# Three more query and key projections by Strassen, ahead of attention, and elementwise sums handed to accumulating DMAs

## The chip, the cores and the metric

The kernel runs on one core of a Trainium2 chip. The metric is the device time of one execution in microseconds, the median of several runs. Before the change it was 1445.59 us (three runs, 1443.7 to 1447.14).

## The reference: what is computed

One layer of a hybrid encoder on x of 1024 tokens by 1024 channels, all in float32: a token mixer with two branches, an output projection and a layer norm, then a SwiGLU network and a second layer norm. The change lies in the mixer:

```python
proj = x @ w_in                       # split into q_a, k_a, v_a, f_a, q_b, f_b, i_b, g_b, gate_a, gate_b
# branch A, 8 heads of 64: causal softmax attention with forget gates
F = cumsum(log_sigmoid(f_a + b_f))
s[t, u] = q_t . k_u / sqrt(64) + F[t] - F[u]      # u <= t
y_a = softmax(s) @ v
# branch B (HGRN2), 4 heads of 128: S_t = diag(f_t) S_(t-1) + k_t v_t^T, o_t = S_t^T q_t
f = lb + (1 - lb) * sigmoid(f_b); q = silu(q_b); k = 1 - f
# then an RMS norm of o, a sigmoid gate, and
merged = sigmoid(gate_a) * (y_a @ w_pa) + sigmoid(gate_b) * (y_b @ w_pb)
mix = merged @ w_o
```

## The kernel before, in words

**Arithmetic.** A product of two float32 matrices is made of three matmuls in the fast format float32r: each operand is split into a high part (a cast by ACT) and a low part (a subtraction by DVE), and high x high, high x low and low x high are summed in PSUM (`mm3`, line 449; `split`, line 420). A unit is one 128x128 block of weights against 512 tokens.

**Strassen.** Large products are made by Winograd's form of Strassen's scheme: of a 2 x 2 block product seven products are made in place of eight, with sums of blocks before and after. The quarters A11 to A22 of x and the sums S1 to S4 are kept as split operands in `vops` (line 489 on). S1 stands in the place of A21, which is restored later (`split4(A21, a21)`).

**Stages.** First the values of both branches (v, Strassen), with the forget gates. Then `qk_first` (line 720) makes queries and keys of head pair 0 by Strassen. Then for each of four pairs `attention(p, qk)` (line 763), and after each of the first three `qk_project` (line 708): the plain product, 8 blocks of 128 channels, for q and for k, in two halves of 512 tokens, each followed by `qk_heads`, which splits the result out of PSUM into q2, k2 and kl for the pair's two heads. After the fourth pair stands `hgrn_project(0)` (line 856), then for four heads `hgrn` (line 884). The gates follow: four plain ones (`gate`, line 1032; PSUM tile gps) and the first halves of others (`gate_part`, line 1047; ge), then the rest by Strassen (gs), the branch outputs' projections (pps), the output projection (o), and the SwiGLU network (fa, fb, fc, then p).

**Attention** of one head: the negated gate sums nf are broadcast by a DMA into one row of box1, and DVE adds the causal constant to a second row (line 773). For each of eight blocks of 128 queries (qb): two matmuls per score chunk, a DVE instruction that adds the gate sums and keeps the minimum, an exponential by ACT that also sums the row, a reciprocal by DVE and a scaling by POOL. After qb 3 and 7 (g = 0, 1) the probabilities are transposed by PE, split again into th and tl, and multiplied by the values (pv).

**HGRN** of one head: fk = f (line 888), its logarithm, running sums b by blocks; then six levels (`level`, line 925) with block lengths from 64 to 2. Each takes the difference e of b and its value at the block's middle (DVE, line 931), two exponentials by ACT, two products by DVE, four matmuls (lp) and a masked copy. `states` (line 971) makes the decayed keys kd likewise from a difference (line 974) and carries the states between blocks.

**Order.** Every call goes through `Plan` (line 57), which does not issue it at once but records it with the tiles it reads and writes and a cost in nanoseconds by engine and size (`cost`, line 131). `schedule` (line 170) then places the calls greedily: of all calls that are ready, the one with the earliest start, ties by a rank of lateness, on five queues (PE, ACT, DVE, POOL, and SP for all DMAs). A tile's buffer is one of a tag's fixed number (`BUFS`, line 378; `SPREAD`, line 30, for PSUM banks), taken in the order of the tag's list. The resulting order of each engine is fixed in the program; on the chip only semaphores hold it. Matmuls of gates and projections thus stand between those of attention and of HGRN wherever the plan found a place. A matmul that depends on another engine is planned with 400 ns of slack (`SLACK`, line 37).

Of the kernel before, what the change touches and what calls it, by code (L numbers as in the profile page):

```python
# [37 lines left out]
SWITCH = 300.0  # L38
ALPHA = 2.0 ** 0.25
# [16 lines left out]

class Plan:
# [4 lines left out]
    OWN = {"PE": 0.0, "ACT": 0.0, "DVE": 127.0, "POOL": 60.0, "SP": 2500.0}  # L62
    SETS = {AF.Exp: 0, AF.Ln: 0, AF.Sigmoid: 1, AF.Silu: 2}

    def __init__(self, tc):
        self.tc = tc
        self.calls, self.tiles, self.log, self.first = [], {}, {}, {}
        self.queues, self.rank = {}, []
        self.early = 0
        self.loose = set()  # L70
# [23 lines left out]
    def add(self, q, method, args, kw):  # L94
        outs, ins = [], []
        flat = list(args) + [v for k, v in kw.items() if k != "accum_out"]
        for i, v in enumerate(flat):
            if isinstance(v, bass.AP):
                (outs if i == 0 else ins).append(v)
        if "accum_out" in kw:  # L100
            outs.append(kw["accum_out"])
        if method == "copy_predicated":
            ins.append(outs[0])
        n = len(self.calls)
        self.rank.append(n - self.early)
        pred = set()
        names = set()
        for writes, aps in ((False, ins), (True, outs)):
            for ap in aps:
                name, b = self.box(ap)  # L110
                bank = str(ap.space).endswith("PSUM")
                names.add(name)
                seen = self.log.setdefault(name, [])
                keep = []
                for e in seen:
                    m, w, c = e
                    hit = c[0] < b[1] and b[0] < c[1] and c[2] < b[3] and b[2] < c[3]
                    if hit and m != n and (w or writes or bank and self.calls[m][0] is not q):
                        pred.add(m)
                    if not (writes and m != n and b[0] <= c[0] and c[1] <= b[1] and b[2] <= c[2] and c[3] <= b[3]):  # L120
                        keep.append(e)
                keep.append((n, writes, b))
                self.log[name] = keep
        fresh = sorted(x for x in names if x in self.tiles)
        for name in fresh:
            self.tiles[name][2] += 1
            self.first.setdefault(name, n)
        both = sum(str(v.space).endswith("SB") and v.free_size() > 128 for v in ins) > 1
        self.calls.append((q, method, args, kw, pred, names, fresh, self.cost(q.name, method, outs, ins, kw), both))

    def cost(self, eng, method, outs, ins, kw):
# [27 lines left out]
        if eng == "POOL":  # L159
            if method == "tensor_tensor" and kw.get("op") == ALU.pow:  # L160
# [9 lines left out]
    def schedule(self, slack, wait):  # L170
# [13 lines left out]
        dma_free = 0.0  # L184
        fifo, slots = {}, {}
# [15 lines left out]
        while done < len(calls):  # L201
            best = None
            for q, av in avail.items():
                for i in av:
# [38 lines left out]
            else:  # L243
# [6 lines left out]
                fin = t + d  # L250
                free[q] = fin
# [35 lines left out]
    def lag(self, i, u, slack):  # L287
        q, uq = self.calls[i][0].name, self.calls[u][0].name
        lat = self.OWN[q] if uq == q else self.LAT[q]
# [4 lines left out]
    def latest(self, slack):  # L294
# [7 lines left out]
        for old, i in self.after:  # L302
            for m in by.get(old, ()):
                users[m].append((i, self.LAT[calls[m][0].name] + 60))
# [62 lines left out]
def trunk(ctx: ExitStack, tc, a: dict, out: bass.AP):  # L367
# [299 lines left out]
    causal = const("causal", [P, 2, P], BF16, "mask")  # L667
# [52 lines left out]
    def qk_first():  # L720

        g, u = (take("hl", [KC, P], f"w{n}0_r") for n in "qk")
        for b, t in enumerate((g, u)):
            sync.dma_start(t, a["w_qk"][b, 0])
        b11, b12, b21, b22 = g[:, :4], u[:, :4], g[:, 4:], u[:, 4:]
        t2 = take("ph", [4, P], "wqk_t2")
        p1, u2, p5 = (half("ph", f"qk0_{i}") for i in ("p1", "u2", "p5"))
        oa, ob, oc = (bank(t, f"qk0_{t}") for t in ("s", "pt", "s"))
        tiles = qk_tiles(0)

        def mul(p, src, o, first):
            T = [take(f"w{x}0" if p in ("p6", "p2", "p7") else "tt", [4, P], f"Tqk{p}{x}", F32R) for x in "hl"]
            split(*T, src)
            more = {} if first else {"skip_group_check": True}
            for c in range(4):
                mm3(o, T[0][:, c], T[1][:, c], vops[p][0][c], vops[p][1][c], first and c == 0, c == 3, more)
# [4 lines left out]
        split4(A21, a21)  # L741
        mul("p1", b11, oa, True)
        act.copy(p1, oa)
        mul("p2", b21, oa, False)
        dve.tensor_sub(t2, b22, b12)
        qk_heads(0, 0, oa, *tiles)
        mul("p6", t2, ob, True)
        dve.tensor_add(u2, ob, p1)
        mul("p3", b22, oc, False)
        dve.tensor_add(u2, oc, u2)  # L750
        qk_heads(1, 0, u2, *tiles)
# [4 lines left out]
        qk_heads(1, 1, p5, *tiles)  # L756
# [3 lines left out]
        qk_heads(0, 1, p1, *tiles)  # L760
        return tiles

    def attention(p, qk):
        q2, k2, kl = qk
        for i in range(2):
# [12 lines left out]
            for qb in range(NT):  # L778
                n = (qb + 1) * P
                pt = full("pf", f"p{h}_{qb}") if qb > 3 else half("ph", f"p{h}_{qb}")  # L780
                soft = small([P, 5], "soft")
                mn, sm, rs = soft[:, :3], soft[:, 3:4], soft[:, 4:]
# [101 lines left out]
    def hgrn(h, qfg, box):  # L884
# [3 lines left out]
        dve.tensor_scalar(fk, fk, olb[:, h:h + 1], lb[:, h:h + 1], op0=ALU.mult, op1=ALU.add)  # L888
# [36 lines left out]
        def level(li):  # L925
# [5 lines left out]
            dve.tensor_sub(e.rearrange("p (n t) -> p n t", t=2 * L), bv,  # L931
                           bv[:, :, L - 1:L].to_broadcast([P, nb, 2 * L]))
# [75 lines left out]
        for hf in range(2):  # L1008
            op = bank("pv", f"op{h}_{hf}")
            ss, rr = (lambda t: (t[:, :4], t[:, 4:]))(small([P, 8], "ss"))  # L1010
# [52 lines left out]
    for p in range(4):  # L1063
        attention(p, qk)
        if p < 3:
            qk = qk_project(p + 1)
# [593 lines left out]
def _constants():  # L1660
    import ml_dtypes
# [3 lines left out]
    causal = np.stack([causal, causal.T], axis=1).astype(ml_dtypes.bfloat16)  # L1665
# [89 lines left out]
```

## Time and profile before

| what | value |
|---|---|
| median of 3 runs | 1445.59 us |
| lowest, highest | 1443.7, 1447.14 us |
| profiled execution, first to last instruction (span) | 1441.5 us |
| mean granted TensorE clock | 0.998 |
| moved by DMA | 181.30 MB, mean 126 GB/s |

The profile records one execution by its span; what lies around the span is not in it, and the median of the runs is 4.1 us longer. In its rows PE is the tensor engine's matmuls and PEld its weight loads, DVE the vector engine, ACT the scalar engine, POOL GpSimd, SP the queue that issues the DMAs. A row of a group gives the operation, output and input tiles by the program's names, shapes, count, then busy time in all and the mean in ns of one, then the idle time of the engine just before these instructions and who ended it. A row of waits gives who waited for whom: microseconds in all, times, longest. All calls are issued at line 363, so rows are told apart by their tiles, not their lines.

### The profile page before, as it was taken

The page shows a single profiled execution, that of the slowest core. Times are in us where ns is not written, and L with a number is a line of the kernel's source. Part 1 is how long each engine was busy: PE and PEld are TensorE (multiplying, and loading weights), DVE is VectorE, ACT ScalarE, POOL GpSimd, SP SyncE. Part 2 cuts the span into 40 slices and gives each one's busy share as a digit, 9 for nine tenths or more (in the row PEclk, how much of TensorE's full clock was granted, in tenths as well). Part 3 has the DMA queues.
Part 4 walks back from the last instruction along what each step waited for, and adds up shares of the span by engine and source line. Part 5 has one row for each costly group of instructions (what it writes and reads, how often), then busy time and mean ns, then how long its engine had stood idle before and what let it go on. Part 6 is the DMA issues. An engine that isn't in the chain of part 4 may idle for free.

```text
span 1441.5 us, 18901 instructions
## 1 busy us (share of the span) xinstructions
PE 1430.0 (99%) x6782; PEld 1188.2 (82%) x6782; DVE 1112.8 (77%) x1952; ACT 668.6 (46%) x1167; POOL 87.2 (6%) x100
## 2 busy tenths in 40 slices
PE   9999999999999999999999999999999999999997
PEld 7788888888888888788888888888888888888886
DVE  8998778567998999845857997666677776798596
ACT  5547768667767663344511443323333334434330
POOL 0002213120100110000000000000000000000011
PEclk9999999999999999999999999999999999999999
DMA  7022212211111455858500233233333326977632
GB/s 270 32 89 67 95 60 74 63 60 51 38 59 46 153 170 164 255 181 290 176 0 2 102 95 124 96 110 110 110 110 110 97 92 201 346 276 235 209 129 85
DMA packets 74029, 181.30 MB, mean 126 GB/s; under 512 B 8384, under 2 KB 9792, under 8 KB 73936
## 3 DMA queue, kind: packets, MB, share of 16 engines
q1 hardware_dynamic: 73936, 180.11, 37.9%
q8 instruction: 53, 0.87, 0.3%
q14 instruction: 40, 0.33, 0.1%
HBM read 139.90 MB, written 40.17 MB: 125 GB/s over the span
## 4 chain that ended last, share of the span: by engine, by line
PE 97%; DVE 2%; DMA 1%; issue 0%; ACT 0%; SPq 0%; DVEq 0%; ACTq 0%
PE p L363 14%; PE fb L363 12%; PE bps L363 9%; PE fc L363 8%; PE fa L363 8%; PE o L363 6%; PE pps L363 6%; PE gs L363 5%; PE vx L363 4%; PE gps L363 3%; PE s L363 2%; PE pv L363 2%; PE qps L363 2%; PE kps L363 2%; PE vy L363 2%; PE pt L363 2%
## 5 line engine op out<-in xcount | busy, mean ns | idle before, releaser
L363 PE MATMUL p<-dp 128*128 128x512 f32 (+1 forms) x957 | 210.1, 382 | 0.0
L363 PEld LDWEIGHTS p<-dp 128*128 128x128 f32 x957 | 175.1, 188 | 34.8
L363 PE MATMUL fc<-xs,Tp 128*128 128x512 f32 x528 | 127.3, 389 | 0.6 <-ACT Tp L363 0.6
L363 PE MATMUL fb<-xs,Tp 128*128 128x512 f32 x528 | 127.2, 389 | 0.0
L363 PEld LDWEIGHTS fc<-xs,Tp 128*128 128x128 f32 x528 | 99.1, 188 | 21.6 <-ACT Tp L363 1.0
L363 PEld LDWEIGHTS fb<-xs,Tp 128*128 128x128 f32 x528 | 99.1, 188 | 20.5
L363 PE MATMUL fa<-x,Tp 128*128 128x512 f32 x480 | 115.6, 389 | 0.0
L363 ACT CAST Tp<-t 128x512 fp32r<-128x512 f32 x88 | 54.2, 619 | 118.8 <-PE fc L363 64.8
L363 DVE TENSOR_TENSOR Tp<-t,Tp 128x512 fp32r<-128x512 f32 x88 | 60.6, 690 | 60.5 <-ACT Tp L363 59.9
L363 PEld LDWEIGHTS fa<-x,Tp 128*128 128x128 f32 x480 | 90.1, 188 | 18.7
L363 PE MATMUL bps<-xh,wb_h 128*128 128x512 f32 x192 | 76.2, 397 | 0.0
L363 PE MATMUL bps<-xl,wb_h 128*128 128x512 f32 x192 | 76.0, 396 | 0.0
L363 PE MATMUL bps<-xh,wb_l 128*128 128x512 f32 x192 | 75.5, 396 | 0.0
L363 POOL TENSOR_TENSOR norm<-norm,mhalf 128x1 f32<-128x1 f32 x16 | 17.2, 1075 | 886.3 <-DVE norm L363 886.3
L363 ACT CAST dp<-dap 128x1024 fp32r<-128x1024 f32 (+1 forms) x42 | 41.0, 979 | 57.8 <-PE p L363 35.7
L363 POOL TENSOR_SCALAR p<-p,soft 128x384 f32<-128x384 f32 (+4 forms) x64 | 51.9, 817 | 261.0 <-DVE soft L363 235.2
L363 DVE TENSOR_TENSOR tl<-pt,th 128x512 fp32r<-128x512 f32 (+1 forms) x96 | 52.2, 554 | 19.7 <-ACT th L363 15.5
L363 ACT CAST th<-pt 128x512 fp32r<-128x512 f32 (+1 forms) x96 | 45.5, 479 | 34.9 <-PE pt L363 30.8
L363 DVE TENSOR_TENSOR dp<-dap,dp 128x1024 fp32r<-128x1024 f32 (+1 forms) x42 | 47.4, 1132 | 15.9 <-ACT dp L363 15.7
L363 PE MATMUL fb<-x,Tp 128*128 128x512 f32 x240 | 57.7, 389 | 0.0
L363 PE MATMUL pt<-ident,p 128*128 128x128 f32 x288 | 53.8, 273 | 0.0
L363 ACT CAST Tp<-wg_r 128x512 fp32r<-128x512 f32 x40 | 24.9, 623 | 62.1 <-PE fb L363 30.2
(565 smaller groups left out, 3476.6 us busy)
## 6 DMA issues: line engine op xcount, KB each, us to landing
dbp<-in_w_fo SPq DMA_DIRECT2D x45, 512.0 KB, 5.3
dap<-a_d SPq DMA_DIRECT2D x35, 512.0 KB, 4.3
wg_r<-in_w_ff SPq DMA_DIRECT2D x22, 512.0 KB, 4.0
wu_r<-in_w_ff SPq DMA_DIRECT2D x22, 512.0 KB, 3.6
a_d<-ar SPq DMA_DIRECT2D x42, 256.0 KB, 2.7
a_d<-as SPq DMA_DIRECT2D x33, 256.0 KB, 3.4
wg_r<-in_w_g SPq DMA_DIRECT2D x16, 512.0 KB, 4.4
sg<-gate_d SPq DMA_DIRECT2D x32, 256.0 KB, 3.4
```

The costliest lines, as they stand in the source:

```text
L363: getattr(q.engine, method)(*args, **kw)
```

## The change

Three things are changed together, and the planner is taught about the new kind of call.

1. `qk_project` is gone. `qk_first` now runs `qk_strassen` for the pairs 1, 2, 3 and 0, one after the other, before the first attention. Pair 0's results go to `qk_heads` as before; those of pairs 1 to 3 are written to the DRAM buffer `qk_d`. Before each later attention `qk_load` reads each half back, twice into one tile so that both halves of the partitions hold it, and ACT and DVE split it.
2. The sums with a broadcast are made by DMAs that add into their destination, issued by POOL: the masked gate sums (SP loads the float32 constant, the DMA adds the gate sums), the decay differences e and the decayed keys' exponents kd (ACT writes the negated broadcast, the DMA adds b).
3. The reciprocals and scalings of the score blocks are gathered: three blocks together, then the fourth. f is made by ACT in place of DVE.

The planner counts 1.0 us of POOL for such a DMA, 2.3 us and the bytes at 200 GB/s until it has landed, and at most three in flight. The core of the diff:

```diff
+RING = 3
+    SOFT, LANDS = 1000.0, 2300.0
+        self.lands.append(self.LANDS + o_bytes(outs[0]) / 200.0 if q.name == "POOL" and method == "dma_start" else 0.0)
...
+                    if self.lands[i]:
+                        t = max(t, ring[-RING])
...
-    causal = const("causal", [P, 2, P], BF16, "mask")
...
-    def qk_project(p):
-        tiles = qk_tiles(p)
-        for b in range(2):
-            plan.early = AHEAD
-            w = weights(a["w_qk"][b, p], [KC, P], f"w{'qk'[b]}{p}", 0)
-            plan.early = 0
-            for hf in range(2):
-                o = bank("g", f"{'qk'[b]}ps{p}_{hf}")
-                project(o, w, hf)
-                qk_heads(b, hf, o, *tiles)
-        return tiles
+    def qk_strassen(p, wtags, btags, tiles=None):
+        g, u = (take(t, [KC, P], f"w{n}{p}_r") for t, n in zip(wtags, "qk"))
...
+        def put(b, hf, o):
+            if tiles:
+                return qk_heads(b, hf, o, *tiles())
+            if o is oa:
+                t = half("gt", f"qk{p}_o")
+                act.copy(t, o)
+                o = t
+            sync.dma_start(qk_d[p, b, :, hs(hf)], o)
...
         mul("p5", b12, oc, True)
         act.copy(p5, oc)
-        split4(A21, a21)
+        if tiles:
+            split4(A21, a21)
...
+    def qk_load(p):
+        q2, k2, kl = qk_tiles(p)
+        for b in range(2):
+            for hf in range(2):
+                for i in range(2):
+                    ot = slice((1 - i) * DH, (2 - i) * DH)
+                    raw = half(f"w{'hl'[i]}0", f"qkr{p}_{b}{hf}{i}")
+                    for j in range(2):
+                        sync.dma_start(raw[j * DH:(j + 1) * DH], qk_d[p, b, i * DH:(i + 1) * DH, hs(hf)])
+                    if b == 0:
+                        act.activation(q2[i][:, hs(hf)], raw, AF.Copy, scale=-0.125)
+                        dve.scalar_tensor_tensor(q2[i][ot, hs(hf)], raw[ot], -0.125, f(q2[i])[ot, hs(hf)],
+                                                 op0=ALU.mult, op1=ALU.subtract)
+                    else:
+                        act.copy(k2[i][:, hs(hf)], raw)
+                        dve.tensor_sub(kl[i][:, hs(hf)], raw, f(k2[i])[:, hs(hf)])
+        return q2, k2, kl
...
+        for p, w, b in ((1, "hl", 0), (2, "kb", 1), (3, "hl", 0), (0, "kb", 1)):
+            qk_strassen(p, (w, w), (("s", "pt", "s"), ("h", "pv", "h"))[b], None if p else tiles)
...
-            for hf in range(2):
-                plain, masked = (nfx[:, b0 + 4 * hf:b0 + 4 * hf + 4].rearrange("p (j c) t -> p j c t", c=2) for b0 in (0, NT))
-                dve.tensor_add(masked, plain, causal[:, None].to_broadcast([P, 2, 2, P]))
+            sync.dma_start(box1[:, r + 1, :], a["causal"])
+            pool.dma_start(box1[:, r + 1, :], nf_d[h].partition_broadcast(P), accum_op=ALU.add)
...
-                dve.reciprocal(rs, sm)
-                pool.tensor_scalar(pt[:, :n], pt[:, :n], rs, 1.0, op0=ALU.mult, op1=ALU.mult)
                 pr.append(pt)
+                if qb % 4 > 1:
+                    lo = 0 if qb % 4 == 2 else 3
+                    dve.reciprocal(sums[:, 4 + lo:5 + qb % 4], sums[:, lo:1 + qb % 4])
+                    for j in range(qb - qb % 4 + lo, qb + 1):
+                        w, rs = (j + 1) * P, sums[:, 4 + j % 4:5 + j % 4]
+                        pool.tensor_scalar(pr[j][:, :w], pr[j][:, :w], rs, 1.0, op0=ALU.mult, op1=ALU.mult)
...
-        dve.tensor_scalar(fk, fk, olb[:, h:h + 1], lb[:, h:h + 1], op0=ALU.mult, op1=ALU.add)
+        act.activation(fk, fk, AF.Identity, scale=olb[:, h:h + 1], bias=lb[:, h:h + 1])
...
-            dve.tensor_sub(e.rearrange("p (n t) -> p n t", t=2 * L), bv,
-                           bv[:, :, L - 1:L].to_broadcast([P, nb, 2 * L]))
+            act.activation(e.rearrange("p (n t) -> p n t", t=2 * L), bv[:, :, L - 1:L].to_broadcast([P, nb, 2 * L]),
+                           AF.Copy, scale=-1.0)
+            pool.dma_start(e, b, accum_op=ALU.add)
...
-            dve.tensor_sub(kd.rearrange("p (c j t) -> p c j t", c=2, t=P), bw,
-                           tot.rearrange("p j c -> p c j")[:, :, :, None].to_broadcast([P, 2, 4, P]))
+            act.activation(kd.rearrange("p (c j t) -> p c j t", c=2, t=P),
+                           tot.rearrange("p j c -> p c j")[:, :, :, None].to_broadcast([P, 2, 4, P]), AF.Copy, scale=-1.0)
+            pool.dma_start(kd, b, accum_op=ALU.add)
...
-            qk = qk_project(p + 1)
+            qk = qk_load(p + 1)
...
-    nc = bacc.Bacc("TRN2", target_bir_lowering=False, num_devices=1, dynamic_dma_scratch_size=256)
+    nc = bacc.Bacc("TRN2", target_bir_lowering=False, num_devices=1, dynamic_dma_scratch_size=512)
```

More of the change, by code (lines that the diff above doesn't have):

```diff
@@ L706, in qk_heads, with mul @@
                 act.copy(kl[i][ot, hs(hf)], f(kl[i])[me, hs(hf)])
[L708 to L722 removed]
+    qk_d = dram.tile([4, 2, P, S], F32, name="qk_d")
+    lanes = [0]
+    def qk_strassen(p, wtags, btags, tiles=None):
+        g, u = (take(t, [KC, P], f"w{n}{p}_r") for t, n in zip(wtags, "qk"))
         for b, t in enumerate((g, u)):
[L724 removed]
+            sync.dma_start(t, a["w_qk"][b, p])
         b11, b12, b21, b22 = g[:, :4], u[:, :4], g[:, 4:], u[:, 4:]
[L726 to L732, printed above, removed]
+        p1, p5 = (half("ph", f"qk{p}_{i}") for i in ("p1", "p5"))
+        oa, ob, oc = (bank(t, f"qk{p}_{t}") for t in btags)
+        def mul(n, src, o, first):
+            lane = lanes[0]
+            lanes[0] ^= 1
+            T = [take(f"w{x}{lane}", [4, P], f"Tqk{p}{n}{x}", F32R) for x in "hl"]
             split(*T, src)
@@ L735, in mul @@
             for c in range(4):
-                mm3(o, T[0][:, c], T[1][:, c], vops[p][0][c], vops[p][1][c], first and c == 0, c == 3, more)
+                mm3(o, T[0][:, c], T[1][:, c], vops[n][0][c], vops[n][1][c], first and c == 0, c == 3, more)
+        def put(b, hf, o):
[6 more added lines that the diff above has]
+            sync.dma_start(qk_d[p, b, :, hs(hf)], o)
         dve.tensor_sub(b12, b12, b11)
@@ L744, in qk_first @@
         mul("p2", b21, oa, False)
+        t2 = take("tt", [4, P], f"wqk{p}_t2")
         dve.tensor_sub(t2, b22, b12)
-        qk_heads(0, 0, oa, *tiles)
+        put(0, 0, oa)
         mul("p6", t2, ob, True)
+        u2 = half("tt", f"qk{p}_u2")
         dve.tensor_add(u2, ob, p1)
```

43 lines of the change are left out of this document (29 added, 14 removed).

## The prediction

> **What bounds the kernel now.** I read the page's busy table first, then what TensorE waited for, then the chain of work that ended last, then busy time by stage.
>
> ```profile
> PE 1430.0 (99%) x6782; PEld 1188.2 (82%) x6782; DVE 1112.8 (77%) x1952; ACT 668.6 (46%) x1167; POOL 87.2 (6%) x100
> PE vy L363 <- DVE mhalf L363: 1.2, 1, 1.2
> PE gs L363 <- DVE gu L363: 1.2, 2, 0.8
> PE fc L363 <- ACT Tp L363: 0.6, 1, 0.6
> 211.19 10.88 PE kps L363 x48
> 89.16 5.44 PE qk_s L363 x24
> ```
>
> TensorE (PE) is busy 1430.0 of 1441.5 us, and its waits for other engines in the whole span are the three rows above, 3.0 us together. A busy PE need not be at its peak, so the chain supplies the rate: 48 key matmuls of 128x512 in 10.88 us and 24 matmuls of pair 0's Strassen in 5.44 us are both 226.7 ns each. The same rate in a long product and in Strassen's short runs of 12 means that a matmul left out is worth 226.7 ns, as long as PE stays fed.
>
> The two stages that the change touches, by windows (PE, PEld, DVE, ACT, POOL, granted clock, DMA share, GB/s), are attention (106 to 328) and HGRN (328 to 540):
>
> ```profile
> 89.00:106.00 17.00, 17.00 (x77) 13.83 (x76) 14.91 (x29) 10.26 (x19) 0.00 (x0) 1.00 0.31 107
> 106.00:328.00 222.00, 221.98 (x1198) 186.76 (x1197) 161.10 (x492) 156.81 (x337) 51.88 (x64) 1.00 0.22 69
> 328.00:540.00 212.00, 212.00 (x1150) 181.97 (x1149) 187.63 (x303) 148.28 (x271) 17.95 (x16) 1.00 0.27 87
> ```
>
> PE is full in all three at granted clock 1.00. In HGRN it is full although VectorE (DVE) is at 187.63/212 = 88%. So 88% on a second engine is a load that this planner has been seen to hide; I use that as the yardstick below. The kernel is bound by the amount of matmul work, and every saving elsewhere is worth nothing by itself.
>
> **The change, part by part.**
>
> *Fewer matmuls.*
>
> ```profile
> L363 PE MATMUL qps<-xl,wq_h 128*128 128x512 f32 x48 | 19.8, 412 | 0.0
> L363 PE MATMUL kps<-xh,wk_l 128*128 128x512 f32 x48 | 18.8, 391 | 0.0
> ```
>
> These are the first and the last of six groups of 48 (the mean of one is longer than the 226.7 ns, since neighbours overlap): 288 matmuls for pairs 1 to 3. By Strassen each pair takes 7 products of 4 blocks of 3 matmuls, 84 instead of 96. 252 instead of 288 leaves out 36 x 0.2267 = **8.2 us**. Nothing else in the diff adds or removes PE work. It moves the 57.1 us of these 252 matmuls ahead of attention.
>
> *The Strassen stage.* Four pairs take 336 matmuls, 76 us of PE, from about 89 us on. No projection can fill in there, since quarter A21 holds a sum until pair 0, now the last, has used it. For each pair DVE has 7 splits, 4 weight sums and 5 combinations, 16 instructions of about 0.69 us (the kl row below), 11 us beside 19 us of PE, and ScalarE (ACT) has some 10 of 0.62 us. Pair 0 ran that way in the first window above with PE full and DVE at 14.91/17. Cost: nothing; PE itself hides it, and if a split is late the next 2.7 us product of another bank goes first. The operands vs2 to vs4 stay in their buffers 57 us longer; behind them wait the first gate weights and the first long score rows. I allow one wait of 1.2 us, the longest row above, at the handover.
>
> *Attention without its projections.*
>
> ```profile
> L363 DVE TENSOR_TENSOR box<-box,causal 128x512 f32<-128x512 f32 x16 | 10.8, 694 | 0.1
> L363 DVE RECIPROCAL soft<-soft 128x1 f32<-128x1 f32 x64 | 10.0, 158 | 4.8 <-ACT p L363 4.5
> L363 DVE SCALAR_TENSOR_TENSOR q<-qps,q 64x512 fp32r<-64x512 f32 x12 | 8.3, 688 | 2.5 <-ACT q L363 2.3
> L363 DVE TENSOR_TENSOR kl<-kps,k 64x512 fp32r<-64x512 f32 x12 | 8.2, 688 | 15.7 <-ACT k L363 15.6
> L363 DVE TENSOR_TENSOR wk_l<-wk_r,wk_h 128x512 fp32r<-128x512 f32 x6 | 4.7, 778 | 6.7 <-ACT wk_h L363 6.6
> L363 DVE TENSOR_TENSOR wq_l<-wq_r,wq_h 128x512 fp32r<-128x512 f32 x5 | 3.4, 689 | 0.7 <-ACT wq_h L363 0.6
> L363 ACT CAST k<-kps 64x512 fp32r<-64x512 f32 x24 | 13.9, 581 | 8.9 <-PE kps L363 7.8 <-DVE kl L363 0.8
> L363 ACT CAST kl<-kl 64x512 fp32r<-64x512 f32 x16 | 9.9, 619 | 2.2 <-DVE kl L363 2.0
> L363 ACT ACTIVATE q<-qps 64x512 fp32r<-64x512 f32 x12 | 7.1, 593 | 3.8 <-DVE q L363 2.2 <-PE qps L363 1.3
> L363 ACT CAST wk_h<-wk_r 128x512 fp32r<-128x512 f32 x6 | 3.7, 625 | 4.2 <-PE qps L363 4.2
> L363 ACT CAST wq_h<-wq_r 128x512 fp32r<-128x512 f32 x5 | 3.1, 617 | 0.3 <-PE kps L363 0.2
> ```
>
> PE keeps 222 - 65.3 = 156.7 us there. DVE loses the mask sums 10.8, half the reciprocals 5.0 and the projection's 8.3 + 8.2 + 4.7 + 3.4, and gains qk_load's 24 x 0.688 = 16.5: 161.1 - 40.4 + 16.5 = 137.2 us, 88% of 156.7. ACT: 156.8 - 37.7 + 24 x 0.62 = 134 us, 86%. That stands exactly at the yardstick, so I cost it at nothing; but it was 73% (161.1/222) before, and the cover is thinner. What covers it is the gates:
>
> ```profile
> L363 PE MATMUL gps<-xh,wg_h 128*128 128x512 f32 x64 | 26.4, 412 | 0.0
> L363 PE MATMUL ge<-xh,we_h x32: 389/393/486, 446.5 to 524.0; 128*128 128x512 f32 x32
> L363 PE MATMUL gps<-xh,wg_l 128*128 128x512 f32 x58 | 23.3, 402 | 0.0
> L363 PE MATMUL bps<-xh,wb_h 128*128 128x512 f32 x17 | 7.0, 413 | 0.0
> L363 DVE TENSOR_TENSOR wg_l<-wg_r,wg_h 128x512 fp32r<-128x512 f32 x8 | 5.5, 690 | 0.0
> L363 DVE TENSOR_TENSOR wb_l<-wb_r,wb_h 128x512 fp32r<-128x512 f32 x3 | 2.1, 690 | 0.8 <-ACT wb_h L363 0.8
> ```
>
> The first two rows stand for three groups each over the whole span, 192 + 96 matmuls, 43.5 + 21.8 = 65.3 us of work that no attention waits for. The other four are attention's window alone: there lay some 59 + 59 + 58 = 176 matmuls of plain gates and 17 + 16 + 16 = 49 of HGRN's first projection, 225 x 0.2267 = 51 us of filler, with 5.5 + 2.1 us of DVE. The 21.8 us of part gates ran from 446 us on, beside the last heads of HGRN. Whether they suffice for both ends is the second rival.
>
> *Recurrence.*
>
> ```profile
> L363 DVE TENSOR_TENSOR box<-hbb 128x1024 f32<-128x1024 f32 x24 | 28.9, 1218 | 0.1
> L363 DVE TENSOR_TENSOR kd<-hbb,tot 128x1024 f32<-128x1024 f32 x4 | 4.9, 1216 | 0.0
> L363 DVE TENSOR_SCALAR hbf<-hbf,lbt 128x1024 f32<-128x1024 f32 x4 | 3.2, 809 | 2.3 <-ACT hbf L363 2.3
> L363 ACT ACTIVATE hbf<-hbf 128x1024 f32<-128x1024 f32 x4 | 4.2, 1062 | 2.0 <-POOL hbb L363 2.0
> L363 ACT ACT_TABLE_LOAD x16 | 20.5, 1283 | 0.3
> L362 ACT ACT_TABLE_LOAD x16 | 20.5, 1283 | 0.3
> ```
>
> DVE loses 28.9 + 4.9 + 3.2 = 37.0 and falls to 150.6 of 212 us (71%). ACT gains 24 + 4 + 4 instructions of 1024 columns at 1.06 us, 33.9 us, and rises to 182.2 of 212 (86%), 41 us of it table loads. So ACT takes DVE's place as the second engine, under the yardstick. I allow one more wait of 1.2 us, in the last head, which has no next projection beside it. If the cover is gone, each microsecond of it is a microsecond of the end.
>
> *The accumulating DMAs.* 24 + 4 in HGRN, 8 in attention, of 512 KB, issued by GpSimd (POOL). The trace of before has none. Nearest rows, KB and us to landing of plain loads, and the waits of POOL's queue:
>
> ```profile
> box<-nf_d SPq DMA_DIRECT2D x8, 512.0 KB, 4.1
> z<-in_x SPq DMA_DIRECT2D x8, 512.0 KB, 8.1
> POOL p L363 <- DVE soft L363: 235.2, 29, 116.1
> L363 POOL TENSOR_SCALAR p<-p,soft 128x384 f32<-128x384 f32 (+4 forms) x64 | 51.9, 817 | 261.0 <-DVE soft L363 235.2
> ```
>
> Bounds: from 4.1 us, the plain load of the same row into the same tile, to 8.1 us, the slowest of this size. I take 5: it is the same tile, with one more read. The planner's own numbers are 2.3 us + 512 KB at 200 GB/s = 4.9. Under 4.1 it gains nothing, since PE is full. A level now goes ACT copy, DMA, two exponentials, but levels use four rows of box1 and three DMAs may be in flight, so a head's seven need about 7 x 6/3 = 14 us of the 53 us that a head takes. Behind an accumulate that waits on POOL stand the scalings of the probabilities and 1 - f, and behind those the transposes on PE. POOL is busy 51.9 us in attention and 17.95 in HGRN, so the issues fit at several microseconds each. [...]
>
> *SP's queue* gets 12 stores of Q and K, 48 loads and 8 mask loads more, and loses 1. They are prefetches beside a DMA share of 0.22 to 0.27 (windows above), and the 17.8 MB that they and attention's accumulates move there are about what attention moves now (222 us x 69 GB/s = 15 MB), so the share about doubles. Cost: nothing.
>
> **Sum.** 1441.5 - 8.2 + 1.2 + 1.2 = 1435.7 us of span. The median of the runs, 1445.6, lies 4.1 us above the profiled span; the same distance gives **1439.8 us**, 0.4% faster.
>
> **Rivals.**
>
> *No stall at all, and the 3.0 us of old waits partly gone*: 1441.5 - 8.2 - 2 + 4.1 = 1435.4. For it: PE waits 0.02 us in 434 us of the two stages now.
>
> *The filler runs short.* Without gates and HGRN's first projection, attention's own DVE work is 137.2 - 7.6 = 129.6 us against 156.7 - 51 = 106 us of PE. At 88% of DVE that stage lasts 147 us: it must eat 41 of the 65.3 us of gates, which leaves 24 us, against the 21.8 and the 16 x 0.2267 = 3.6 us of plain gates that HGRN used. It just about balances. If 5 to 9 us are missing, the gain is gone: about 1445.5. For it: the greedy order puts any ready matmul on an idle PE, and attention comes first. Against: two of the six buffers of tag qk are free beside pair 3, so 96 matmuls, 22 us, of HGRN's first projection can run there.
>
> *Late landings, slower.* PE's order is fixed when the program is built, for landings of 4.9 us. If an accumulate takes longer, the level's matmuls stand at the head of PE's queue and everything waits. Levels come in bursts of three (the three in flight), so with the state step there are about 3 bursts for each of 4 heads: 12 x the lateness. Slower begins beyond 8.2/12 = 0.7 us of lateness, so at landings of 5.6 us. At 6.5 us, between my value and the slowest row, it costs 12 x 1.6 = 19 us: 1445.6 - 8.2 + 19 = 1456. For it: loads of 512 KB spread from 4.1 to 8.1 us. Against: a head leaves room, and other matmuls were ordered ahead by 0.4 us of slack only in the plan, often more in fact. [...]
>
> *The change does not save matmuls in fact*: excluded by the counts, 288 against 252.
>
> **How the numbers follow.** Chances: forecast 0.60, no stall 0.04, filler short 0.16, late landings 0.20. A measurement of this kernel tells about 0.2%, 2.9 us, from no change: below 1442.7 is faster, above 1448.5 slower. Faster: 0.60 + 0.04 and a little of the second rival, 0.65; same: most of that rival, 0.12; slower: the late landings and its far end, 0.23. The range runs from 1435.5, the case without stalls, to 1452: it holds the short filler and the late landings up to 1.2 us (12 x 1.2 - 8.2 = +6.2), which leaves out some 0.15.
>
> **What would show it.** Right: 252 matmuls of the query and key products at 226.7 ns before about 165 us, PE's waits under 6 us, attention's window near 157 us, DVE near 71% and ACT near 86% in HGRN. Wrong: PE idle beside lp or kdt released by ACT after a landing of over 5.6 us (late landings), or PE idle with gates all done by the middle of HGRN (short filler), or PE idle in the Strassen stage on DVE or ACT splits.

## The result, and the profile after

| what | before | after |
|---|---|---|
| median | 1444.64 us | 1488.53 us (1487.24 to 1490.15) |
| ratio, with its 95% interval | | 1.0302 [1.0285, 1.0318] |
| span of the profiled execution | 1441.5 us | 1486.7 us |
| mean granted clock | 0.998 | 0.988 |

The change made the kernel 43.9 us slower; I had forecast 1439.8, faster. (The median of before is that of four runs here, one more than ahead of the prediction.) First the busy table of the changed kernel's page, then its busy time by stage (columns as before: PE, PEld, DVE, ACT, POOL, granted clock, DMA share, GB/s). The Strassen stage is 89 to 165, attention 165 to 325, HGRN 325 to 580.

```profile
PE 1438.2 (97%) x6746; PEld 1187.6 (80%) x6746; DVE 1089.9 (73%) x1908; ACT 685.5 (46%) x1189; POOL 111.9 (8%) x136
```

```profile
89.00:165.00 76.00, 75.09 (x333) 61.90 (x333) 46.45 (x77) 28.19 (x51) 1.97 (x2) 1.00 0.42 128
165.00:325.00 160.00, 155.46 (x869) 130.27 (x868) 132.43 (x418) 126.07 (x290) 52.93 (x66) 0.99 0.54 157
325.00:580.00 255.00, 224.28 (x1169) 187.37 (x1168) 157.86 (x280) 176.30 (x305) 41.95 (x48) 0.95 0.49 121
...
370.00:380.00 10.00, 2.67 (x10) 1.85 (x9) 1.58 (x3) 5.56 (x9) 0.86 (x1) 0.74 0.70 165
...
420.00:430.00 10.00, 3.58 (x10) 2.59 (x9) 3.63 (x5) 3.59 (x6) 2.87 (x3) 0.63 0.56 105
```

The first two stages are nearly as forecast: TensorE idles 0.9 us in the Strassen stage and 4.5 in attention. HGRN is not: TensorE idles 30.7 of 255 us, in holes such as 370 to 380, where DVE is busy 1.58 and ACT 5.56 of 10 us, so no engine is the bound there. Over the whole span the 36 matmuls fewer took away 8.2 us, the idle time rose from 11.5 to 48.5 (+37.0), and TensorE was busy 1438.2 us where 1430.0 - 8.2 = 1421.8 was due (+16.4): -8.2 + 37.0 + 16.4 = 45.2, the difference of the spans. Most of the 16.4 are matmuls at a lower clock: an estimate from the two mean granted clocks is (0.998 - 0.988) x 1486.7 = 14.9 us. What they look like, in the timeline of PE around the hole at 370 (start, duration, instruction, idle time before it and its releaser):

```profile
370.55 0.39 PE L378 MATMUL bps<-xl,wb_h 128*128 128x512 f32 x1
370.77 0.39 PE L378 MATMUL bps<-xh,wb_l 128*128 128x512 f32 x1
378.50 0.80 PE L378 MATMUL dg<-qkh,once 128*128 128x512 f32 x1 [7.33 <-ACT hbg L378]
379.09 0.63 PE L378 MATMUL dg<-qkl,once 128*128 128x512 f32 x1
379.51 0.63 PE L378 MATMUL dg<-qkh,once 128*128 128x512 f32 x1
```

After 7.3 us without work the matmuls start 0.42 us apart (379.09, 379.51), where they started 0.22 apart (370.55, 370.77). The granted clock is 0.50 from 378 to 380, 0.59 from 380 to 382 and 1.00 from 382 to 384. This hole cost its own 7.3 us and then some: behind the one at 378.50 the next seven starts, up to 381.65, took 3.15 us, where 0.2267 us each would make 1.59.

Who made the holes: the changed kernel's waits (us in all, times, longest), then POOL's timeline in one stretch of the last head, then its DMA issues (count, KB each, median us to landing).

```profile
POOL box L378 <- issue: 71.4, 14, 8.3
...
ACT box L378 <- DMA box<-hbb: 36.0, 16, 4.5
...
DVE ob L378 <- POOL ss L378: 21.4, 4, 8.9
```

```profile
538.03 0.91 POOL L378 DMA_DIRECT2D box<-hbb  x1 [2.88 <-issue]
542.99 0.88 POOL L378 DMA_DIRECT2D box<-hbb  x1 [4.04 <-issue]
547.82 0.86 POOL L378 DMA_DIRECT2D box<-hbb  x1 [3.95 <-issue]
552.68 0.89 POOL L378 DMA_DIRECT2D box<-hbb  x1 [4.01 <-ACT hbg L378]
```

```profile
box<-hbb POOLq DMA_DIRECT2D x24, 512.0 KB, 4.6
...
box<-nf_d POOLq DMA_DIRECT2D x8, 512.0 KB, 6.5
```

An accumulate of the recurrence lands in 4.6 us, close to the 5 that I had taken; the masks' eight, which read nf from DRAM, take 6.5. But the next one in the recurrence starts only when the one before has landed, 4.8 to 5.0 us later, and for 4 us of that POOL waits on "issue", that is, it waits on nothing that the profile shows. The plan had ordered all engines for three in flight. The third wait shows who else stands in POOL's queue: the states' scaling (ss), then DVE, then the states on PE.

### The profile page after: what moved, and what is told of

Its sections match the earlier page's. It is cut to its first block, busy times and chain, and to the rows that moved or that the text cites. A ratio compares the mean times of both kernels' runs of the same rounds, so it can differ in the third digit from the quotient of the medians.

```text
span 1486.7 us, 19069 instructions
## 1 busy us (share of the span) xinstructions
PE 1438.2 (97%) x6746; PEld 1187.6 (80%) x6746; DVE 1089.9 (73%) x1908; ACT 685.5 (46%) x1189; POOL 111.9 (8%) x136
## 4 chain that ended last, share of the span: by engine, by line
PE 81%; DMA 7%; issue 6%; DVE 3%; ACT 2%; POOL 1%; SPq 0%; DVEq 0%; ACTq 0%; POOLq 0%
PE p L378 14%; PE fb L378 11%; PE fc L378 8%; PE fa L378 8%; PE o L378 6%; PE pps L378 6%; PE vx L378 4%; PE gs L378 3%; PE bps L378 3%; PE vy L378 2%; DMA box<-hbb 2%; PE gps L378 2%; PE s L378 2%; PE pv L378 2%; DMA qkr<-qk_d 2%
## 5 line engine op out<-in xcount | busy, mean ns | idle before, releaser
L378 POOL TENSOR_TENSOR norm<-norm,mhalf 128x1 f32<-128x1 f32 x16 | 14.9, 932 | 888.5 <-DVE norm L378 888.5
L378 POOL TENSOR_SCALAR p<-p,sums 128x640 f32<-128x640 f32 (+5 forms) x64 | 51.9, 840 | 108.4 <-DVE sums L378 58.6
L378 DVE TENSOR_TENSOR dp<-dap,dp 128x1024 fp32r<-128x1024 f32 (+1 forms) x42 | 47.4, 1132 | 15.0 <-ACT dp L378 14.9
L378 ACT ACTIVATE p<-p,soft 128x640 f32<-128x640 f32 (+6 forms) x64 | 49.9, 783 | 5.8 <-DVE soft L378 5.6
```

The lines of the kernel that those rows point to most:

```text
L378: getattr(q.engine, method)(*args, **kw)
```

## The experiments

My theory after the trace, **queue**: the scratch space that the program sets aside for DMAs (`dynamic_dma_scratch_size`, 512 bytes in the changed kernel) takes one such DMA at a time. Rivals: **generation**, POOL itself needs the 5 us to issue one; **filler**, the second rival of the prediction, that attention eats the gates that HGRN's end needs; **late landings**, which the 4.6 us above speak against. The kernel before ran beside all that follow, at 1444.1 to 1444.7 us, and the ratios are to it.

**1 and 2. The disputed DMA by itself**, six accumulates of 512 KB, six of 256 KB and six plain copies, back to back on POOL, with 512 and with 4096 bytes.

> Six accumulating DMAs of 512 KB, six of 256 KB and six plain copies of 512 KB, SBUF to SBUF, issued one after the other by GpSimd with nothing else to do, and the changed kernel's 512 bytes of descriptor scratch; the output is not the layer's. Theory ring (the scratch holds the descriptors of one such accumulate only, so the next one is issued when the one before has landed): starts of the 512 KB accumulates about 4.9 us apart, of the 256 KB ones closer by what the shorter transfer lands earlier, of the plain copies closer still (fewer descriptors, so more of them fit). Rival generation (GpSimd takes some 4.9 us to write the descriptors of one accumulate): 4.9 us apart for both sizes, since the number of rows is the same.

> The same kernel with 4096 bytes of descriptor scratch. Theory ring: the 512 KB accumulates start about 1 us apart, the busy time that one issue shows on GpSimd. Rival generation: 4.9 us apart as with 512 bytes.

POOL's timeline, with 512 bytes and then with 4096:

```profile
14.97 0.86 POOL L26 DMA_DIRECT2D acc<-b  x1 [4.52 <-issue]
20.46 0.88 POOL L26 DMA_DIRECT2D acc<-b  x1 [4.62 <-issue]
...
44.56 0.87 POOL L28 DMA_DIRECT2D hal<-b  x1 [2.75 <-issue]
48.14 0.88 POOL L28 DMA_DIRECT2D hal<-b  x1 [2.70 <-issue]
...
58.98 1.07 POOL L30 DMA_DIRECT2D cpy<-b  x2 [2.22 <-issue]
```

```profile
4.70 5.45 POOL L26 DMA_DIRECT2D acc<-b  x6 [4.26 <-DMA b<-in_x]
```

With 512 bytes they stand 5.4 to 5.5 us apart (3.6 for half the size); with 4096 six are issued in 5.45 us, 0.9 each. Generation is refuted: an issue takes POOL 0.9 us, and room decides. What fills the room, descriptors as the theory had it or something else, and how many bytes one accumulate takes, no run shows; the 896 bytes of the next run were chosen as room for three before a run had shown it. With 4096 bytes ten accumulates are issued (six of 512 KB, four of 256 KB) before the eleventh waits 2.43 us for an earlier one to land. Not explained: of the plain copies of the 512-byte run some followed each other at once (the last row, two in 1.07 us).

**3. Room for three in the changed kernel** (two small tiles change their buffers to make space, and the plan's order shifts a little with them). The line of the edit that counts, shortened:

```diff
-    nc = bacc.Bacc("TRN2", ..., dynamic_dma_scratch_size=512)
+    nc = bacc.Bacc("TRN2", ..., dynamic_dma_scratch_size=896)
```

> The changed kernel with 896 bytes of descriptor scratch in place of 512 (two small tiles share other buffers to make the room), everything else and the plan the same. Theory ring: three accumulates can be in flight as the plan assumes; GpSimd's accumulates in the recurrence come up to 1 us apart, the four holes of 7 to 10 us in TensorE go, the recurrence's window shrinks from 255 to about 215 us and the time falls to 1437 to 1445 us. Rival generation: no difference, 1485 to 1491 us. Rival filler (TensorE runs out of matmuls that wait for nothing): the spacing falls, but the holes stay and the time stays over 1470 us.

1461.68 us (1459.99 to 1466.44), 1.0120 [1.0096, 1.0144]. POOL's timeline, and the landing:

```profile
358.28 2.71 POOL L378 DMA_DIRECT2D box<-hbb  x3 [6.97 <-issue]
```

```profile
box<-hbb POOLq DMA_DIRECT2D x24, 512.0 KB, 6.5
```

Three are now issued together, and 26.8 of 43.9 us come back. The queue theory wanted all of it back; 17 us were left, for which it had no cause. Together in flight they land in 6.5 us in place of 4.6.

**4. The other two parts of the change alone**: Strassen for all pairs, the gathered reciprocals and f on ACT; the sums on DVE as before.

> The changed kernel with its accumulating DMAs undone: masked gate sums, decay differences and decayed keys are DVE subtractions and additions again; Strassen for all pairs, the gathered reciprocals and the gate value on ACT stay. Theory ring and rival generation (the loss lies in the accumulating DMAs alone): TensorE stays fed, 36 matmuls fewer show, 1436 to 1443 us. Rival filler: the attention without its projections and the recurrence without spare gates starve TensorE whoever makes the sums, 1450 us or more.

1449.72 us, 1.0031 [1.0019, 1.0043]: slower than before, although 36 matmuls are gone and no accumulate is left. Where the gates ran (count, shortest/median/longest in ns, from when to when), and the windows where TensorE idled:

```profile
L378 PE MATMUL ge<-xh,we_h x32: 389/394/497, 275.1 to 525.0; 128*128 128x512 f32 x32
```

```profile
520.00:530.00 10.00, 8.30 (x47) 6.34 (x46) 9.56 (x17) 3.25 (x12) 0.00 (x0) 1.00 0.71 238
530.00:540.00 10.00, 7.30 (x40) 5.39 (x38) 9.10 (x18) 6.34 (x20) 3.76 (x2) 1.00 0.04 17
```

The part gates (ge) ran from 446.5 us before and now from 275.1: attention, without its projections, took them. At HGRN's end, 520 to 540, nothing is left to put beside DVE at 9.56 and 9.10 of 10. That is the filler rival: not that the filler is too little in all, but that attention takes it first.

**5. The accumulating DMAs**, on the projections of before (the gathered reciprocals and f on ACT stay here too).

> The kernel before with the accumulating DMAs, the gathered reciprocals and the gate value on ACT, at 512 bytes of scratch; queries and keys of pairs 1 to 3 by the plain product between the attentions, as before. Theory ring: the recurrence waits for accumulates issued one per landing whatever stands ahead of it, so most of the 39 us between the changed kernel (1488.5) and Strassen alone (1449.7) show here too: 1470 to 1485 us. Rival: the accumulates only hurt because Strassen took the spare matmuls; then this run is within 10 us of the kernel before, 1440 to 1455 us.

1485.74 us, 1.0294 [1.0278, 1.0309]. By stage (attention, HGRN's middle and its end):

```profile
106.00:328.00 222.00, 221.97 (x1194) 186.16 (x1193) 151.61 (x444) 156.94 (x333) 53.67 (x70) 1.00 0.33 96
...
360.00:500.00 140.00, 120.92 (x640) 102.68 (x639) 87.25 (x150) 101.92 (x166) 21.62 (x26) 0.94 0.51 115
500.00:560.00 60.00, 49.58 (x262) 41.56 (x262) 33.23 (x56) 36.65 (x67) 9.23 (x11) 0.94 0.68 176
```

The mechanism is as expected, the time 0.7 us above the range: 41.7 us, and nearly all of the holes lie in HGRN. Attention with the masks' DMAs is full, 221.97 of 222; this comes back below.

**6. The true number told to the planner**, 512 bytes as in the changed kernel.

```diff
-RING = 3
+RING = 1
```

> The changed kernel with RING = 1 in the planner, so that the plan issues an accumulate only when the one before has landed, which is what the 512 bytes allow on the chip. Theory ring: the order then fits the chip, the long waits at the head of GpSimd's and TensorE's queues shrink, and the time falls well below 1488 us, to 1455 to 1470; it does not reach Strassen alone (1449.7), since seven accumulates of 5 us take 35 us of each head's about 50. Rival (the serial accumulates themselves are too slow for the recurrence, whatever the order): 1480 us or more.

1463.26 us (1458.72 to 1468.64), 1.0140 [1.0112, 1.0167]: within the range. HGRN's middle and end:

```profile
360.00:500.00 140.00, 140.00 (x755) 119.92 (x754) 98.94 (x171) 126.19 (x195) 27.19 (x32) 1.00 0.62 140
500.00:560.00 60.00, 52.37 (x290) 44.86 (x289) 52.59 (x91) 35.47 (x88) 8.96 (x9) 0.94 0.60 163
```

With the same one DMA at a time the middle is full, because other matmuls were ordered into the gaps, and 25.3 us come back. So most of the 26.8 us was not the slow queue itself but an order made for a faster one. The end stays short, 52.37 of 60.

**7. The part gates held back**, on the kernel of experiment 4: their weights' loads get a made-up dependence on the stores of the last pair's results. The core of the edit:

```diff
+        plan.must = held_of[0]
         w = weights(a["w_g"][i, fb], [KC, P], f"we{n}", lane)
+        plan.must = set()
...
+    held_of[0] = {i for i, c in enumerate(plan.calls) if c[1] == "dma_start" and any(x.startswith("ya3_") or "ya6_" in x or "ya7_" in x for x in c[5])}
```

> Strassen alone (as in the run without accumulating DMAs) with the four part gates, 96 matmuls or 21.8 us of TensorE work, held back by a made-up dependence until the last attention's results are stored. Theory filler: the hole of some 5 us of TensorE at the recurrence's end goes, and the time falls from 1449.7 by 3 to 5 us if attention does not need these gates; if attention needs them, as much appears there and the time stays within 2 us. Rival late loads (the rest of the loss comes from the reloads of queries and keys on SP's queue in attention): no more than 2 us of difference, with attention's stalls unchanged.

**1439.1 us** (1438.41 to 1442.77), 0.9966 [0.9956, 0.9976]: faster than both kernels, and 10.6 us below experiment 4, twice what I expected. The gates, the stages, and the loads of queries and keys:

```profile
L380 PE MATMUL ge<-xh,we_h x32: 387/392/478, 348.9 to 519.4; 128*128 128x512 f32 x32
```

```profile
165.00:325.00 160.00, 158.39 (x908) 132.96 (x907) 143.23 (x442) 130.08 (x296) 58.27 (x64) 1.00 0.33 106
325.00:360.00 35.00, 35.00 (x173) 29.57 (x172) 27.76 (x43) 26.50 (x40) 1.10 (x2) 1.00 0.22 68
360.00:500.00 140.00, 140.00 (x769) 120.27 (x768) 122.71 (x200) 96.22 (x179) 13.26 (x12) 1.00 0.24 77
500.00:580.00 80.00, 79.92 (x396) 66.80 (x395) 75.61 (x123) 35.75 (x75) 2.73 (x2) 1.00 0.56 172
```

```profile
qkr<-qk_d SPq DMA_DIRECT2D x48, 128.0 KB, 2.9
```

HGRN is full, and attention loses 1.6 us. Against the kernel before, TensorE's busy time falls by 6.2 us where the 36 matmuls alone are 8.2.

**8. Half of the Strassen stage**: pairs 1 and 0 ahead, pairs 2 and 3 plain, so that 192 matmuls of projection stay in attention; sums on DVE, gates free.

> Strassen ahead of attention for pair 1 only besides pair 0; pairs 2 and 3 by the plain product between the attentions as before; sums by DVE. 12 matmuls fewer than before (2.7 us) and 192 matmuls of projection left in attention. Theory filler: TensorE stays fed, 1440 to 1443.5 us, faster than the kernel before. Rival (what Strassen ahead costs is at the handover to attention and in the operands held longer, with one pair as with three): no gain, 1445 us or more.

The filler theory's range was missed: 1448.17 us, 1.0034 [1.0020, 1.0048], which lies in the rival's.

```profile
L378 PE MATMUL ge<-xh,we_h x32: 387/393/478, 294.0 to 523.0; 128*128 128x512 f32 x32
```

```profile
520.00:530.00 10.00, 8.39 (x46) 6.65 (x46) 9.77 (x20) 4.19 (x13) 1.69 (x1) 1.00 0.43 145
```

I had thought that more filler in attention would leave the gates for the end. It does not: the greedy order starts them at 294 and the end is short again (8.39 of 10). So more filler in attention does not by itself leave any for HGRN's end. This does not account for the whole miss: TensorE idles 2.6 us in all of 325 to 580, and over the span it idles 3.3 us more than in the kernel before and is busy 1.3 us longer with 12 matmuls fewer. The rival's cause, the operands held longer and the handover to attention, was not tried by itself.

**9. The control**: the kernel before, with the gates held.

> The kernel before with the part gates held until the last head pair's results are stored, nothing else. In the kernel before these gates ran from 446.5 us on anyway, behind that point, and TensorE's order comes out the same; only one weight load moves. If holding is worth 10.6 us because of what the Strassen stage takes away, it is worth nothing here: 1443 to 1447 us. If holding were a gain by itself, about 1435 us.

1444.55 us, 0.9999 [0.9988, 1.0010], as expected. Holding is worth nothing by itself; in the kernel before the gates came late anyway.

**10 and 11. Holding on top of experiments 3 and 6.**

> The kernel after with room for three accumulating DMAs (896 bytes) and the part gates held. Three-losses theory (queue, gates spent early, late landings): from 1461.7 us without holding it falls by about the 10.6 us that holding gave with the sums on VectorE, to 1449 to 1454 us; what is left above 1439 us is the cost of the accumulates with room in the queue, 6.5 us from issue to landing beside the plan's 4.9. If the room in the queue was all that mattered, 1458 to 1463 us. If accumulates with room and gates in place are as good as VectorE, 1437 to 1441 us.

> The kernel after with the plan told that one accumulate is in flight (1463.3 us) and the part gates held. If the two losses add, it falls by about 10.6 us to 1450 to 1455 us. If the gates are what covers the waits for single accumulates in the recurrence, it falls more, to 1442 to 1448 us, since 96 matmuls more stand there. If holding only moves the hole into attention, it stays at 1460 to 1466 us.

1459.47 us, 1.0094 [1.0077, 1.0111], and 1459.33, 1.0092 [1.0073, 1.0110]: 2.2 and 3.9 us gained in place of 10.6. For both my adding theory missed; for the first, the time is the one expected if only the room mattered. Both stand some 20 us above 1439.1, and held gates do not remove that. The next three runs look for the cause.

**12. Of the accumulates the masks' eight alone**, on the kernel of experiment 7, with 512 bytes.

> Strassen with gates held (1439.1 us), and of the accumulating DMAs only the eight for the masked gate sums; the recurrence on VectorE. If these eight cost nothing: 1437.5 to 1441 us. If the masks' DMAs are part of the loss in attention, about 0.7 us for each of eight: 1443 to 1446 us.

Missed by both: 1451.10 us (1446.93 to 1455.60), 1.0038 [1.0023, 1.0053], so 12.0 us for eight DMAs and the loads of the constant that they add to. Attention by window, one of its holes in the timeline, the waits in attention, and the loads of queries and keys:

```profile
165.00:325.00 160.00, 152.40 (x860) 127.45 (x859) 134.27 (x424) 126.65 (x290) 60.44 (x70) 0.99 0.49 147
```

```profile
200.05 1.14 ACT L380 CAST k<-qkr 128x512 fp32r<-128x512 f32 x2 [3.99 <-DMA qkr<-qk_d]
201.10 0.47 ACT L380 CAST th<-pt 128x384 fp32r<-128x384 f32 x1
...
201.62 0.44 PE L380 MATMUL pv<-th,vhl 128*128 128x384 f32 x1 [2.71 <-ACT th L380]
```

```profile
ACT q L380 <- DMA qkr<-qk_d: 5.2, 3, 2.4
PE pv L380 <- ACT th L380: 5.1, 4, 2.7
...
ACT k L380 <- DMA qkr<-qk_d: 4.4, 2, 4.0
```

```profile
qkr<-qk_d SPq DMA_DIRECT2D x48, 128.0 KB, 4.8
...
box<-nf_d POOLq DMA_DIRECT2D x8, 512.0 KB, 6.9
```

The chain can be read off: the reloaded keys land late, ACT waits 3.99 us on them, the split th stands behind it in ACT's queue, and the values' matmul on PE waits for th. Each of PE's four waits for th comes within 1.6 us of the end of such a wait of ACT. In experiment 7 these loads' median is 2.9 us and ACT waits on none of them; here it is 4.8, and ACT waits 9.6 us on five. The share of the DMA engines rises from 0.33 to 0.49. POOL's queue is not the cause here: POOL waits 0.3 us on "issue" in attention, PE waits for none of its scalings, and with room for three (experiment 10) TensorE is as short there, 152.39 of 160. Of the 12.0 us, TensorE's idle time in attention explains 7.6 - 1.6 = 6.0; the rest is spread over other stages and was not taken apart.

Two limits of this reading. In experiment 5 the same eight DMAs cost nothing in attention, where no queries and keys come by DMA; but the projections are still there to fill, so that run does not tell which of the two helped. And the median landing is not the whole measure: in experiment 4, without any accumulate, ACT waits 5.0 us on the loads in attention, and in experiment 6, with the eight, 14.2 us, both at a median of 2.9. So the loads have little lead in some orders anyway, and the accumulates make it worse.

**13. Which of the masks' transfers**: the constant is still loaded, DVE adds.

> Strassen with gates held; the masks' float32 constant is still loaded 512 KB for each of eight heads by the SP queue, but VectorE adds the gate sums (one instruction of 1024 columns) in place of the accumulating DMA. If the accumulates delay the loads of queries and keys, as their landings of 7.3 us beside them suggest: back near 1439 us, 1438 to 1442, and queries' and keys' landings near the 2.9 us of the run without them. If the constant's own loads and SP's issues do it: 1447 to 1452 us, landings near 4.8 us. Half and half would be near 1445.

1441.22 us, 0.9975 [0.9965, 0.9986]. The accumulates make 9.9 of the 12.0 us, the constant's loads with DVE's longer addition 2.1. The loads of queries and keys:

```profile
qkr<-qk_d SPq DMA_DIRECT2D x48, 128.0 KB, 3.6
```

**14. Of the accumulates the recurrence's 28 alone**, with room for three.

> Strassen with gates held; masks by VectorE; the 28 accumulating DMAs of the recurrence with room for three in flight (896 bytes). If the parts add, 8.4 us above 1439.1 (what they added on top of the masks' DMAs): 1446 to 1450 us, with TensorE idle in the recurrence alone. If the two kinds of accumulates cost only together: 1438 to 1442 us.

1449.33 us, 1.0030 [1.0019, 1.0040]: 10.2 us, within what adding gave. By window and by landing:

```profile
350.00:360.00 10.00, 7.42 (x41) 5.97 (x40) 7.86 (x12) 7.33 (x13) 1.40 (x2) 1.00 0.98 218
...
390.00:400.00 10.00, 9.87 (x46) 7.76 (x44) 4.91 (x8) 7.84 (x13) 2.49 (x3) 1.00 1.07 238
```

```profile
box<-hbb POOLq DMA_DIRECT2D x24, 512.0 KB, 8.2
```

In such stretches the DMA engines are full (share 0.98 and 1.07), at 218 to 238 GB/s, and an accumulate lands after 8.2 us, beside gate weights that come at the same time. ACT waits 20.3 us on these landings in HGRN. TensorE's idle time there, 7.7 us from 325 to 580, is 0.1 in experiment 7.

## Why the prediction was wrong, point by point

The kernel of experiment 7 ran at 1439.1 us, near my number. From there the way to the result can be walked in steps, each between two medians:

| step | us |
|---|---|
| Strassen for all pairs, sums on DVE, gates held (7) | 1439.1 |
| + masks by accumulating DMAs, with the loads of their constant, 512 bytes (12) | +12.0 = 1451.1 |
| + recurrence by accumulating DMAs, with room for three (10) | +8.4 = 1459.5 |
| + gates not held (3) | +2.2 = 1461.7 |
| + room for one, plan for three (the change) | +26.8 = 1488.5 |

Measured against the kernel before that ran beside each, the four steps are 11.4, 8.4, 2.2 and 26.9 us. Taken in another order they would come out otherwise: holding the gates is worth 10.6 us without accumulates and 2.2 with them.

- **Matmuls, -8.2 us: nearly right.** The 36 matmuls are gone. In experiment 7 TensorE is busy 1423.8 us, 6.2 under before, and idles 1.4 us more. That this run's 1439.1 us lies so near my 1439.8 is partly luck: it has no accumulates and holds its gates, which is not the kernel that I forecast.
- **The Strassen stage costs nothing: right within 1 us.** 76.00 of 76 us in experiment 7, 75.09 in the changed kernel.
- **"Three DMAs may be in flight, so a head's seven need about 7 x 6/3 = 14 us": this step failed**, and it is the largest, 26.8 us. I took three from the planner's constant, which is a statement about the program and no row of a trace. One was in flight: seven at 4.9 us are 34 us. My sum had two waits of 1.2 us; TensorE's idle time rose by 37.0, and 30.7 us of it lie in HGRN. I had bounded the landing from both sides (4.1 to 8.1) and not the number in flight. "Issues fit at several microseconds each" was true and beside the point: POOL had time, but what stood behind a blocked issue did not. That most of it comes back either with more room (1461.7) or with the right number in the plan (1463.3) shows that what cost so much was a difference between plan and chip. Either remedy still leaves the kernel 17 to 19 us slower than before, so this step is not the only one that failed.
- **Landings of 5 us: right for one in the recurrence, wrong for three and for the masks.** 4.6 us one at a time, 6.5 in experiment 3 and 8.2 in 14; the masks' eight took 6.5 in the changed kernel, though the plain load of the same row, my nearest row, had taken 4.1. I used both "three in flight" and "5 us" in one product; the runs show that they exclude each other. The slower rival, late landings, had slower begin at 5.6 us and gave 1456 at 6.5; experiment 14, with 8.2, lost 10.2 us against 7. So the rival's mechanism is in there (ACT waits on landings, TensorE idles), but 12 times the lateness would have been 38 us, which is too high. Landings grow with the number in flight also in experiments 1 and 2, where nothing of the layer runs: a median of 5.1 us one at a time, and of 11.5 for six issued together with more behind them; POOL issues them at 0.9 us each.
- **SP's queue and the DMA share, "cost: nothing": wrong**, by up to 12.0 us on the kernel of experiment 7; in the changed kernel itself TensorE idles 4.5 us in attention. I saw that the share of the DMA engines in attention would about double (0.22 before, 0.54 in the changed kernel) and called the loads prefetches. They are, but with too little lead, and ACT takes them in order. The mean share of 0.54 holds a stretch of 10 us at 0.92 (185 to 195).
- **Attention at 88% and HGRN at 86% of the second engine, "cost nothing": half right.** Experiment 7 bears it out for attention, with DVE at 143.23 of 160 (90%) and TensorE at 158.39. For ACT in HGRN experiment 6 does so in the middle: ACT is at 126.19 of 140 (90%) with TensorE full. But the yardstick came from a stage that had filler. Where the filler is gone it doesn't hold: experiment 4 idles 5.1 us at 520 to 550, and is 10.6 us slower in all than with the gates held.
- **The filler rival was real.** I gave it 0.16 and 1445.5 us; alone it made 1449.7. My count of it, 24 us against 25.4, balanced to 1.4 us, and I read that as enough; it left out that the greedy order does not save filler for the stage that lacks it.
- **What I had not in the sum**: the clock. Of the 45.2 us, 16.4 are longer busy time, most of it matmuls slowed after holes (14.9 by the mean clocks). After the hole of 7.3 us the rows show 0.42 us from start to start in place of 0.22, and a granted clock of 0.50 from 378 to 380 and 1.00 again from 382 on.

What stays open: why experiment 10 gained only 2.2 us from holding the gates while experiment 7 gained 10.6; how the 10.2 us of experiment 14 divide between late landings and ACT's 28 added copies; the half of experiment 12's 12.0 us that is not idle time in attention; and most of experiment 8's miss. The gathered reciprocals and f on ACT were in every run of the whole layer but 9 and were never tried alone.

## What to carry to other kernels

Before a planner's constant enters a forecast as a fact (how many transfers are in flight, how long one takes), look for a row that shows it, or bound it like any unknown cost; when the plan and the chip differ, a fixed order turns the difference into holes (26.8 us here). Transfers that cost little by themselves may delay each other (here queries and keys landed in 4.8 us in place of 2.9 beside the masks' DMAs), so ask what lead each has and look at the stretches where the DMA engines are full and not at their mean. And where work is taken out of a stage that was full, ask what the scheduler will put there and which later stage needed that work.

## What the runs showed of the hardware that was not expected

- Accumulating DMAs of 512 KB from POOL, 128 rows: one in flight with 512 bytes of scratch space (5.4 to 5.5 us apart, alone), three issued together with 896, six with 4096 and four more of 256 KB behind them before one waited. In the changed kernel a blocked issue held what stood behind it on POOL, and the profile books it as waiting for "issue" (71.4 us in 14 waits; DVE waited 21.4 us on POOL's ss).
- POOL is busy about 0.87 us per accumulate. Landings: in the recurrence 4.6 us one at a time, 6.5 to 8.2 with three; from DRAM beside the loads of attention 6.5 in the changed kernel and 6.9 in experiment 12, one at a time; by themselves a median of 11.5 for six issued together with more behind them.
- After a hole of 7.3 us matmuls of 128x512 started 0.42 us apart in place of 0.22, and the granted clock in windows of 10 us with long holes, or just behind one, was 0.63 to 0.92 in six (370 to 390, 420 to 440, 480 to 490, 540 to 550) and 1.00 in two (470 to 480, 530 to 540).
